# A decoder block on one core: the indexer gets two steps per z tile, and the modulation's loads move from the z tiles to the output projection

## The chip, the core and the metric

One Trainium2 chip, one core. TensorE (PE) does the matmuls, VectorE (DVE), ScalarE (ACT) and GpSimd (POOL) the rest; SyncE (SP) issues the DMAs. Each engine takes its instructions in its own order and waits where an operand isn't there. The metric is the device time of one launch in microseconds (us), the median of several runs.

## The reference, cut

256 tokens, width 2048, all in float32. Only what the change touches is shown.

```python
idx_score = einsum(w_idx, relu(einsum(q_idx, k_idx)))        # the indexer, 16 heads
_, sel = lax.top_k(where(causal, idx_score, -inf), top_k)    # top_k = 64
logits = q_lat @ kv_sel + bias                               # attention over the selected keys, 16 heads
z, xbc, dt_raw, g_a, g_b = split(h @ w_in)                   # z: 4096 columns
y = ssd(conv(xbc), dt) ; y = rms_norm(y * silu(z))
merged = sigmoid(g_a) * (y_a @ w_proj_a) + sigmoid(g_b) * (y_b @ w_proj_b)
x1 = x + gate1 * (merged @ w_out)
x2 = x1 + gate2 * swiglu(norm(x1) * (1 + scale2) + shift2)
# the six modulation vectors (gates, scales, shifts) are silu(c) @ w_ada + b_ada: 2048 x 12288
```

The selection is done here as a mask: eight rounds of "take the 8 largest of a row, strike them out" (MAX and MATCH_REPLACE), and what was struck out stays.

## The kernel before, in words

**Jobs.** The program is a list of jobs, each with one 1 MB weight tile. A tile is loaded into one of a few `raw` buffers (L144, on SP), split into a high part `wh` (ScalarE, L196) and the remainder `wl` (VectorE, L197), and multiplied on TensorE: `wh` against both parts of the activations side by side (L278, 512 columns) and `wl` against the high part (L280, 256 columns). Loads run three buffers ahead, splits two jobs ahead (`AHEAD`). Four PSUM accumulators and four side banks turn over. The scheduler of the framework sets each engine's order from the order of the code and its own estimate.

**Side work.** `gens` holds generators; a job calls `advance()` `ticks` times, spread over its matmuls (L161), and each call takes one step of each generator. The indexer, `index_gen` (L727), starts with the first z tile: eight steps of a pair of heads (`ix`, L737 and L739; relu L742; weighted sums L745 and L747), one for the causal mask on GpSimd (L752, L753), four of two top-k rounds (L758, L759), and a last one (L762, then L763 and L764 on GpSimd). The attention pairs open with a `drain` of what is left of it (`open_a2`, L595).

**Stages around the change.** Nine z tiles (`ZLEAD`, columns of z; z0 to z8) go ahead of the attention pairs. Then pair j (its q, k, v) and a z tile take turns, eight times. The two heads of a pair come one job later: logits `lg` (L873, L874), GpSimd adds mask and bias (L877, L878; the bias is loaded by L915 into `t1` from a table in DRAM), maxima L883, exponentials L886 on ScalarE, scaling L890, transposes `pT` (L894). A z tile is emptied by ScalarE (L296) and VectorE (`zs`, L297), gated with L860 and L861 (`zt`), and stored (L862, `d_z`). Later follow the projection of the attention (pa), convolution and state-space groups (cv) with the first part of their projection (pb), the rest of pb, and the output projection (out0 to out15). In the last pb jobs VectorE merges each of 16 blocks with L1180 and L1181, and with L300 and L301 (`mg`) makes the operand of the output projection; out0's matmuls take the blocks in turn, and so wait for the last `mg`.

**Granules of the modulation.** 48 of the weight tiles of `w_ada` (1 MB each, a "granule") are taken by VectorE, not TensorE: each half of a tile is scaled by a value of silu(c) and added to `acc2` (L556; the first half of a group starts it with L554). Eight granules make half a vector; after the eighth, `finish` sums over the partitions with 8 products of 128x1 on TensorE (L534; the trace has 16 records, since each is taken in two passes) and adds the bias (L537). `add_bg` puts a granule into the list of loads after a job; `Spread(jobs, n)` spreads n of them over a stage, by the table `BG`: lead, pairs, pa, convolution, pb. What is left then goes behind the out jobs, at most one each here. A granule takes a `raw` buffer as a weight tile does.

Of the kernel before, what the change touches and what calls it, by code (L numbers as in the profile page):

```python
# [22 lines left out]
NLEAD = 4  # L23
ONPE = (0, 1, 2, 3, 8, 10, 12)
AHEAD = 2
BG = (4, 8, 8, 24, 4)
SSD_LAG = 3
OUTC = ((0, 1), (1, 2), (2, 4), (12, 14), (4, 6), (6, 8), (14, 16), (8, 10), (10, 12))
OUTP = 12
# [20 lines left out]
def hybrid_block_kernel(  # L50
# [242 lines left out]
    def evac(acc, dst):  # L293

        lo = tmp.tile([P, L], F32, tag="ev", name="ev", bufs=3)
        act.activation(lo, acc[:, L:], AF.Copy)  # L296
        dve.tensor_tensor(dst, acc[:, :L], lo, op=ALU.add)  # L297
# [273 lines left out]
    def full(key, src, post, **kw):  # L571
        product_jobs(key, [src], [(0, k) for k in range(KT)], hr, lambda m, acc: post(acc), **kw)
# [282 lines left out]
    def add_z(j, ticks=1):  # L855
        def post(acc):
            v = tmp.tile([P, L], F32, tag="zv", name="zs")
            evac(acc, v)
            th = tmp.tile([P, L], F32, tag="zt", name="zt")
            act.activation(th, v, AF.Tanh, scale=0.5)  # L860
            dve.scalar_tensor_tensor(th, th, 1.0, v, op0=ALU.add, op1=ALU.mult)  # L861
            nc.sync.dma_start(d_z[j], th)  # L862

        full(f"z{j}", w_z[j], post, ticks=ticks, wide=True)
# [267 lines left out]
    def add_pb(q, mp, pre=None, ticks=1):  # L1132
        def post(m, acc):
            pb = B["pb"][:, m]
            if q == 0:
                act.activation(pb, acc, AF.Copy)
                return
            if q < 3:
                dve.tensor_tensor(pb, acc, pb, op=ALU.add)
                if q == 2:  # L1140
                    merge_most(m, pb)
            else:
                merge(m, pb, acc)

        def rhs(k):
            g = 2 * q + k // 4
            while g not in B["done"]:
                advance()
            return B["y"][g][:, k % 4]

        order = [(2 * mp + m, k) for m in range(2) for k in range(8)]
        product_jobs(f"pb{q}_{mp}", [w_pb[8 * q + mp]], order, rhs, post, pre=pre, ticks=ticks, pref=merge_load if q >= 2 else None)
# [161 lines left out]
    zs = iter(range(32))  # L1314
# [11 lines left out]

    sp = Spread(ZLEAD, BG[0])
    for i in range(ZLEAD):
        add_z(next(zs))
        sp()  # L1330
    first_pair = len(jobs)
    sp = Spread(28 - ZLEAD, BG[1])
    for j in range(8):
# [4 lines left out]
    for _ in range(12 - ZLEAD):  # L1338
        add_z(next(zs))
        sp()  # L1340
    sp = Spread(16, BG[2])
    for m in range(16):
# [3 lines left out]
    nz = 20  # L1346
    sp = Spread(48, BG[3])
    for g in range(8):
# [9 lines left out]
        if g >= 4:  # L1358
            add_pb(*next(pbs))
    sp = Spread(16, BG[4])  # L1360
    for q, mp in pbs:
# [156 lines left out]
```

## Time and profile before

| | |
|---|---|
| median of 3 runs | 1997.14 us (1996.43 to 1997.53) |
| profiled execution | 2000.2 us, span 1998.5 us |
| granted TensorE clock | 0.995 |
| TensorE busy | 98% of the span |
| VectorE, ScalarE busy | 73%, 53% |

Rows of the trace give the start of an instruction or of a run of equal ones, its duration, the engine, the line, the tiles (output<-inputs, buffer numbers left out) and in brackets the idle time ahead of it and what ended that. Instructions that follow each other overlap by some 0.08 us on VectorE, and TensorE's matmuls more, so the time from start to start is the work's pace. Sums of the forecast are made against the profiled execution's own times.

### The profile page before, as it was taken

The numbers are of one execution on the slowest core, as the hardware profiler recorded it, in microseconds if no ns is written. First come the engines' busy times: TensorE is split into PE (matmuls) and PEld (weight loads), VectorE is DVE, ScalarE is ACT, GpSimd is POOL, SyncE is SP. The second block draws the span as 40 slices with busy tenths as digits, with TensorE's granted clock in tenths as the row PEclk, the third lists the DMA queues.
The fourth block names the chain that finished last, engine by engine and source line by source line (L and its number), as shares of the span: only waits on it lengthen the run. The fifth ranks groups of instructions, "written<-read, shape, count | busy, mean of one in ns | idle before, by whom it ended". The sixth has DMA issues, their size and how long they took to land.

```text
span 1998.5 us, 31817 instructions
## 1 busy us (share of the span) xinstructions
PE 1968.4 (98%) x12990; PEld 1788.4 (89%) x12990; DVE 1455.4 (73%) x1804; ACT 1053.5 (53%) x1408; POOL 150.9 (8%) x145
## 2 busy tenths in 40 slices
PE   8999999999999999999999999999999999999997
PEld 7999998899888888999999988888888888888887
DVE  6877677977778999988889865668786555544443
ACT  3556755565345766666664344544444444443432
POOL 0000000310000111110114211000000000000000
PEclk9999999999999999999999999999999999999998
DMA  9888667666897677766767876467775555565552
GB/s 394 352 319 329 247 241 264 232 234 241 298 337 259 251 253 265 271 254 225 265 241 245 284 253 216 166 229 272 264 288 217 190 190 190 200 216 195 190 184 90
DMA packets 101650, 492.29 MB, mean 246 GB/s; under 512 B 10464, under 2 KB 45648, under 8 KB 46592
## 3 DMA queue, kind: packets, MB, share of 16 engines
q1 hardware_dynamic: 99840, 486.19, 67.2%
q0 software_dynamic: 704, 3.15, 0.4%
q8 instruction: 102, 1.67, 0.3%
q10 hardware_dynamic: 960, 0.92, 0.1%
q14 instruction: 44, 0.36, 0.0%
HBM read 475.44 MB, written 17.92 MB: 247 GB/s over the span
## 4 chain that ended last, share of the span: by engine, by line
PE 81%; issue 9%; DVE 5%; ACT 1%; DMA 1%; POOL 1%; SPq 1%; DVEq 0%; POOLq 0%; ACTq 0%
PE acc_gu L278 15%; PE acc_gu L280 8%; PE acc_dn L278 8%; PE acc_cv L278 7%; PE acc_z L278 4%; PE acc_dn L280 4%; PE acc_cv L280 4%; PE acc_pa L278 3%; PE acc_out L278 3%; PE cyc L826 2%; PE cyc L825 2%; PE cyc L824 2%; PE acc_z L280 2%; DVE wl L197 2%; PE acc_pa L280 1%
## 5 line engine op out<-in xcount | busy, mean ns | idle before, releaser
L197 DVE TENSOR_TENSOR wl<-raw,wh 128x2048 fp32r<-128x2048 f32 (+1 forms) x325 | 731.4, 2252 | 318.0 <-ACT wh L196 309.5
L196 ACT ACTIVATE wh<-raw 128x2048 fp32r<-128x2048 f32 (+1 forms) x325 | 605.3, 1865 | 307.4 <-PE acc_dn L278 94.9
L278 PE MATMUL acc_gu<-h,wh 128*128 128x512 f32 x1312 | 313.1, 391 | 0.0
L278 PEld LDWEIGHTS acc_gu<-h,wh 128*128 128x128 f32 x1312 | 241.1, 188 | 46.7
L278 PE MATMUL acc_cv<-h,wh 128*128 128x512 f32 x768 | 189.2, 396 | 0.0
L556 DVE SCALAR_TENSOR_TENSOR acc<-raw,cact,acc 128x1024 f32<-128x1024 f32 x120 | 160.1, 1334 | 20.4 <-DMA raw<-in_ada_dram 19.8
L280 PEld LDWEIGHTS acc_gu<-h,wl 128*128 128x128 f32 x1312 | 168.2, 191 | 6.4
L280 PE MATMUL acc_gu<-h,wl 128*128 128x256 f32 x1312 | 170.2, 283 | 0.0
L278 PEld LDWEIGHTS acc_cv<-h,wh 128*128 128x128 f32 x768 | 140.5, 188 | 29.1 <-issue 1.7
L278 PE MATMUL acc_dn<-ffact,wh 128*128 128x512 f32 x660 | 160.0, 392 | 0.0
L826 PE MATMUL cyc<-h,wl 128*128 128x256 f32 x512 | 144.8, 285 | 0.9 <-DVE wl L197 0.8
L824 PE MATMUL cyc<-h,wh 128*128 128x256 f32 x512 | 145.5, 285 | 0.0
L825 PE MATMUL cyc<-h,wh 128*128 128x256 f32 x512 | 145.3, 285 | 0.0
L236 PE MATMUL acc_pb<-y,wh 128*128 128x256 f32 x512 | 143.9, 281 | 1.3 <-DVE sgr L1180 1.3
L237 PE MATMUL acc_pb<-y,wh 128*128 128x256 f32 x512 | 143.0, 279 | 0.0
L238 PE MATMUL acc_pb<-y,wl 128*128 128x256 f32 x512 | 142.8, 279 | 0.0
L278 PEld LDWEIGHTS acc_dn<-ffact,wh 128*128 128x128 f32 x660 | 120.2, 188 | 23.1
L278 PE MATMUL acc_z<-h,wh 128*128 128x512 f32 x512 | 123.5, 393 | 0.0
L278 PEld LDWEIGHTS acc_z<-h,wh 128*128 128x128 f32 x512 | 93.8, 188 | 20.9 <-issue 2.7
L280 PEld LDWEIGHTS acc_cv<-h,wl 128*128 128x128 f32 x768 | 98.7, 191 | 4.4 <-issue 0.5
L280 PE MATMUL acc_cv<-h,wl 128*128 128x256 f32 x768 | 101.0, 283 | 0.0
L826 PEld LDWEIGHTS cyc<-h,wl 128*128 128x128 f32 x512 | 98.3, 193 | 1.5 <-DVE wl L197 1.5
(345 smaller groups left out, 3316.0 us busy)
## 6 DMA issues: line engine op xcount, KB each, us to landing
raw<-in_w_gu_dram SPq DMA_DIRECT2D x88, 1024.0 KB, 4.8
raw<-in_ada_dram SPq DMA_DIRECT2D x79, 1024.0 KB, 5.3
raw<-in_w_ssm_dram SPq DMA_DIRECT2D x48, 1024.0 KB, 4.8
raw<-in_w_dn_dram SPq DMA_DIRECT2D x44, 1024.0 KB, 4.7
raw<-in_w_z_dram SPq DMA_DIRECT2D x32, 1024.0 KB, 5.0
raw<-in_w_pb_dram SPq DMA_DIRECT2D x32, 1024.0 KB, 5.0
raw<-in_w_s_dram SPq DMA_DIRECT2D x30, 1024.0 KB, 5.9
raw<-in_w_pa_dram SPq DMA_DIRECT2D x16, 1024.0 KB, 6.1
```

The costliest lines, as they stand in the source:

```text
L196: act.activation(whf[:, o], raw[:, o], AF.Copy)
L197: dve.tensor_tensor(wlf[:, o], raw[:, o], whf[:, o].bitcast(F32), op=ALU.subtract)
L236: pe.matmul(acc, wh, rhs[:, :L], start=first, stop=False)
L237: pe.matmul(acc, wh, rhs[:, L:], start=False, stop=False)
L238: pe.matmul(acc, wl, rhs[:, :L], start=False, stop=last)
L278: pe.matmul(acc, wh[:, t], rhs(k), start=n == 0, stop=False, skip_group_check=True)
L280: pe.matmul(acc[:, :L], wl[:, t], rhs(k)[:, :L], start=False, stop=n == end, skip_group_check=True)
L556: dve.scalar_tensor_tensor(a, r, cact[:, k : k + 1], a, op0=ALU.mult, op1=ALU.add)
L824: pe.matmul(acc, wh[:, t], h[:, k, :L], start=first, stop=False, skip_group_check=True)
L825: pe.matmul(acc, wh[:, t], h[:, k, L:], start=False, stop=False, skip_group_check=True)
L826: pe.matmul(acc, wl[:, t], h[:, k, :L], start=False, stop=(c == n - 1), skip_group_check=True)
```

## The change

`BG[0]` goes from 4 to 0, and each of the nine z tiles of the lead takes two steps of the side work, where it took one. Since the 48 granules stay, each one moves four places later in the list, and the last four, for which BG has no room any more, are placed by the loop over the out jobs, behind out0 to out3.

```diff
-BG = (4, 8, 8, 24, 4)
+BG = (0, 8, 8, 24, 4)
...
     sp = Spread(ZLEAD, BG[0])
     for i in range(ZLEAD):
-        add_z(next(zs))
+        add_z(next(zs), ticks=2)
         sp()
```

The loop that places the last ones, unchanged:

```python
    for m in range(16):
        add_out(m)
        if m < 15:
            n = len(bg)
            add_bg(-(-n // (15 - m)))
```

In the changed kernel the indexer's 14 steps end with z7. Three places show what moves; numbers at the names are buffers, and the brackets name the engines or DMA queues that an instruction waits for.

TensorE and VectorE at the end of the lead, the changed kernel. First z9's matmuls, before and then changed; then VectorE from the last step of the indexer (L762) to the split for z10 (`wl87`); `zs_3626` empties z8.

```order
L278 MATMUL acc_z9_0_3732<-h_130,wh88_3545 128x512 [waits Activation_49]
...
L278 MATMUL acc_z9_0_3716<-h_130,wh84_3589 128x512 [waits DVE_49]
L278 MATMUL acc_z10_0_3854<-h_130,wh87_3712 128x512 [waits Activation_49]
...
L762 TENSOR_SCALAR sc_134<-sc_134 128x384 [waits DVE_49]
L197 TENSOR_TENSOR wl83_3543<-raw83_3403,wh83_3542 128x2048 [waits DMAHW4_49]
L861 SCALAR_TENSOR_TENSOR zt_3536<-zt_3536,zs_3532 128x256 [waits DMAHW7_49,Activation_49]
L197 TENSOR_TENSOR wl84_3590<-raw84_3474,wh84_3589 128x2048 [waits DMAHW6_49,PE_49,Activation_49]
L297 TENSOR_TENSOR zs_3579<-acc_z7_0_3546,ev_3580 128x256 [waits Activation_49]
L861 SCALAR_TENSOR_TENSOR zt_3583<-zt_3583,zs_3579 128x256 [waits DMAHW1_49,Activation_49]
L554 TENSOR_SCALAR acc2_0_0_3707<-raw86_3587,cact_108 128x1024 [waits DMAHW5_49]
L556 SCALAR_TENSOR_TENSOR acc2_0_0_3707<-raw86_3587,cact_108,acc2_0_0_3707 128x1024 [waits DVE_49]
L297 TENSOR_TENSOR zs_3626<-acc_z8_0_3593,ev_3627 128x256 [waits Activation_49]
```

Before, L762 stood behind `zs` of z8 and the split of z9, and no granule stood between `zs` of z7 and that of z8. z9's first matmul now waits for VectorE where it waited for ScalarE.

SP at the same place: before, from the load of pair 0's neighbour (`raw88`, z9) on, then the changed kernel from its load of pair 1 (`raw85`) on.

```order
L144 DMA raw88_3478<-in_w_z_dram 128x2048 [waits DMAHW7_49,DMAHW3_49,DVE_49]
L144 DMA raw89_3482<-in_w_att_dram 128x2048 [waits DMAHW6_49,DVE_49]
L862 DMA d_z_122<-zt_3413 128x256 [waits DMAHW5_49,DVE_49]
L144 DMA raw90_3543<-in_ada2_dram 128x2048 [waits DMAHW1_49,DVE_49]
...
L144 DMA raw85_3540<-in_w_att_dram 128x2048 [waits DMAHW2_49,DVE_49,Activation_49]
L862 DMA d_z_122<-zt_3470 128x256 [waits DMAHW1_49,DVE_49]
L915 DMA part_142<-d_tz_129 128x2x256 [waits Pool_49]
L915 DMA part_142<-d_tz_129 128x2x256 [waits DMAHW3_49,Pool_49]
L862 DMA d_z_122<-zt_3536 128x256 [waits DMAHW4_49,DVE_49]
L144 DMA raw86_3587<-in_ada2_dram 128x2048 [waits DMAHW5_49,Activation_49]
```

The two L915 (biases of pairs 2 and 3) stood behind four more loads before; now they stand ahead of the first granule's, `raw86`, and wait for GpSimd, which must have used the biases of pairs 0 and 1.

VectorE at the end of pb, the changed kernel, from the merge of blocks 10 and 11 (`sgr_11719`, `sgr_11746`) to the last `mg`; `raw255` is granule 4 of the last group, `raw257` granule 5, `wl254` the split of out0, `wl256` that of out1 (in parts).

```order
L1181 TENSOR_TENSOR pbacc_5935<-pbacc_5935,sgr_11746 128x256 [waits DVE_49,Pool_49]
L556 SCALAR_TENSOR_TENSOR acc2_1_1_10883<-raw255_11781,cact_108,acc2_1_1_10883 128x1024 [waits DMAHW6_49]
L301 TENSOR_TENSOR mg_11374<-pbacc_5935,mg_11374 128x256 [waits Activation_49] x2
L197 TENSOR_TENSOR wl254_11788<-raw254_11713,wh254_11787 128x2048 [waits DMAHW4_49]
...
L1181 TENSOR_TENSOR pbacc_5935<-pbacc_5935,sgr_11818 128x256 [waits DVE_49,Pool_49]
L556 SCALAR_TENSOR_TENSOR acc2_1_1_10883<-raw255_11781,cact_108,acc2_1_1_10883 128x1024
L301 TENSOR_TENSOR mg_11374<-pbacc_5935,mg_11374 128x256 [waits Activation_49] x2
L197 TENSOR_TENSOR wl256_11860<-raw256_11785,wh256_11859 128x512 [waits DMAHW7_49]
...
L1181 TENSOR_TENSOR pbacc_5935<-pbacc_5935,sgr_11896 128x256 [waits DVE_49,Pool_49]
L556 SCALAR_TENSOR_TENSOR acc2_1_1_10883<-raw257_11853,cact_108,acc2_1_1_10883 128x1024 [waits DMAHW6_49]
L301 TENSOR_TENSOR mg_11374<-pbacc_5935,mg_11374 128x256 [waits Activation_49] x2
```

None of the three L556 stood in this stretch before; the L534 and L537 of the group, which did, are now in out3, behind two of its matmuls.

## Rows read from the trace of the kernel before

**Rows 1.** The page: busy time, share of the span, instructions.

```profile
PE 1968.4 (98%) x12990; PEld 1788.4 (89%) x12990; DVE 1455.4 (73%) x1804; ACT 1053.5 (53%) x1408; POOL 150.9 (8%) x145
```

**Rows 2.** What TensorE waited for: us in total, times, longest.

```profile
PE acc_out L278 <- DVE mg L301: 1.5, 2, 1.3
...
PE py L1097 <- DVE ar L1060: 1.0, 1, 1.0
```

**Rows 3.** Timeline of TensorE from z7 to pair 2: start, duration; z7 (with one index step), z8 (with none), pair 0, z9, z10, the transposes, a q of pair 2.

```profile
342.23 3.94 PE L278 MATMUL acc_z<-h,wh 128*128 128x512 f32 x16
...
348.86 3.94 PE L278 MATMUL acc_z<-h,wh 128*128 128x512 f32 x16
...
354.55 0.28 PE L236 MATMUL acc_q<-cqs,wh 128*128 128x256 f32 x1
...
360.21 3.80 PE L278 MATMUL acc_z<-h,wh 128*128 128x512 f32 x16
...
372.73 3.80 PE L278 MATMUL acc_z<-h,wh 128*128 128x512 f32 x16
...
380.51 0.33 PE L894 MATMUL pT<-ident,part 128*128 128x128 f32 x1 [0.77 <-DVE part L890]
381.26 0.90 PE L894 MATMUL pT<-ident,part 128*128 128x128 f32 x5 [0.42 <-DVE part L890]
...
384.47 0.38 PE L236 MATMUL acc_q<-cqs,wh 128*128 128x256 f32 x1 [0.90 <-DVE mx L883]
```

**Rows 4.** Timeline of VectorE in the same stretch.

```profile
348.17 2.29 DVE L197 TENSOR_TENSOR wl<-raw,wh 128x2048 fp32r<-128x2048 f32 x1 [1.78 <-ACT wh L196]
350.38 1.40 DVE L747 SCALAR_TENSOR_TENSOR sc<-rl,wi,sc 128x128 f32<-128x128 f32 x4
...
352.03 0.72 DVE L758 MAX8 m<-sc 128x8 f32<-128x128 f32 x2
...
353.64 0.61 DVE L758 MAX8 m<-sc 128x8 f32<-128x128 f32 x2
...
354.81 0.61 DVE L758 MAX8 m<-sc 128x8 f32<-128x128 f32 x2
...
367.12 0.35 DVE L762 TENSOR_SCALAR sc<-sc 128x384 f32<-128x384 f32 x1
367.39 2.29 DVE L197 TENSOR_TENSOR wl<-raw,wh 128x2048 fp32r<-128x2048 f32 x1
```

**Rows 5.** Timeline of GpSimd: the causal mask, the last mask, and the bias adds of heads 0, 1 and 3.

```profile
351.46 0.47 POOL L752 TENSOR_SCALAR_AFFINE_SELECT sc<-sc 128x128 f32<-128x128 f32 x1 [116.69 <-DVE sc L747]
...
367.54 2.28 POOL L763 TENSOR_SCALAR_AFFINE_SELECT sc<-sc 128x128 f32<-128x128 f32 x1 [15.26 <-DVE sc L762]
369.78 0.39 POOL L764 TENSOR_SCALAR_AFFINE_SELECT sc<-sc 128x256 f32<-128x256 f32 x1
370.15 0.45 POOL L877 TENSOR_TENSOR part<-part,sc 128x128 f32<-128x128 f32 x1
370.57 0.74 POOL L878 TENSOR_TENSOR part<-part,sc 128x256 f32<-128x256 f32 x1
...
373.92 2.78 POOL L878 TENSOR_TENSOR part<-part,sc 128x256 f32<-128x256 f32 x1
```

**Rows 6.** Timeline of TensorE from `finish` in pb to out3.

```profile
1143.98 1.84 PE L534 MATMUL ada<-ones,acc 128*128 128x1 f32 x16
...
1156.41 0.51 PE L278 MATMUL acc_out<-mg,wh 128*128 128x512 f32 x1 [0.19 <-DVE mg L301]
1158.21 0.50 PE L278 MATMUL acc_out<-mg,wh 128*128 128x512 f32 x1 [1.29 <-DVE mg L301]
...
1170.14 3.84 PE L278 MATMUL acc_out<-mg,wh 128*128 128x512 f32 x16
```

**Rows 7.** Timeline of VectorE at the end of pb.

```profile
1143.22 0.75 DVE L1180 SCALAR_TENSOR_TENSOR sgr<-sgr,acc_pb 128x256 f32<-128x256 f32 x2
...
1146.08 2.29 DVE L197 TENSOR_TENSOR wl<-raw,wh 128x2048 fp32r<-128x2048 f32 x1 [1.43 <-ACT wh L196]
1148.29 0.75 DVE L301 TENSOR_TENSOR mg<-pbacc,mg 128x256 fp32r<-128x256 f32 x2
...
1152.63 1.89 DVE L197 TENSOR_TENSOR wl<-raw,wh 128x512 fp32r<-128x512 f32 x3
...
1157.74 0.42 DVE L301 TENSOR_TENSOR mg<-pbacc,mg 128x256 fp32r<-128x256 f32 x1
```

**Rows 8.** Timeline of SP's issues: in the pairs, and at the end of pb (the load at 1140.13 and the next are those of out1 and out2).

```profile
377.42 0.46 SPq L144 DMA_DIRECT2D raw<-in_w_att_dram  x1
...
1140.13 3.24 SPq L144 DMA_DIRECT2D raw<-in_w_out_dram  x2
```

**Rows 9.** DMA issues: count, KB each, median us from issue to landing. Each row is of a window with one granule or one weight tile: issued at 343.85 and 394.21 (behind two L915) in the lead and the pairs, and at 1140.13 (out1).

```profile
raw<-in_ada_dram SPq DMA_DIRECT2D x1, 1024.0 KB, 5.0
...
raw<-in_ada_dram SPq DMA_DIRECT2D x1, 1024.0 KB, 7.5
...
raw<-in_w_out_dram SPq DMA_DIRECT2D x1, 1024.0 KB, 7.1
```

**Rows 10.** All L554 of the program: min/median/max duration in ns.

```profile
L554 DVE TENSOR_SCALAR acc<-raw,cact x8: 743/746/753, 293.1 to 1424.1; 128x1024 f32<-128x1024 f32 x8
```

**Rows 11.** Timeline of VectorE near 1060.

```profile
1056.93 1.28 DVE L556 SCALAR_TENSOR_TENSOR acc<-raw,cact,acc 128x1024 f32<-128x1024 f32 x1
...
1061.80 2.83 DVE L197 TENSOR_TENSOR wl<-raw,wh 128x2048 fp32r<-128x2048 f32 x1
```

**Rows 12.** Timeline of ScalarE: its half of the split of out0.

```profile
1144.13 1.91 ACT L196 ACTIVATE wh<-raw 128x2048 fp32r<-128x2048 f32 x1 [2.90 <-PE acc_pb L237]
```

## The prediction

> **What bounds the kernel now.** The page's busy times come first: TensorE (PE) works 1968.4 of 1998.5 us, no other engine nearly as long [rows 1]. So a change counts only where TensorE waits or gets other work. Next the waits of TensorE: the longest outside the program's start is at the end of the mixer, where `acc_out` waits for the merged tile `mg` of L301 [rows 2], and three more stand together at the start of the attention pairs. Then the timeline at these places.
>
> In the pairs, `pT` is held twice (0.77 and 0.42 us) by L890 of VectorE (DVE) and `acc_q` once (0.90) by L883 [rows 3]. VectorE's rows say why: the top-k rounds, 1.17 us each, start only at 352.03, after the last z of the lead, and L762, which ends them, stands at 367.12 [rows 4]. The mask then goes through GpSimd (POOL): L763, L764, and two bias adds a head from 370.15 on [rows 5]. In the nine z tiles themselves TensorE shows no wait: z8 starts at 348.86, pair 0 at 354.55, z9 at 360.21 [rows 3].
>
> In the output projection TensorE reaches the last two blocks of out0 before `mg` is there (waits of 0.19 and 1.29); the last `mg` starts on VectorE at 1157.74 and TensorE's block at 1158.21 [rows 6, 7].
>
> **The change, part by part.** The instructions are the same ones (no matmul is added or dropped); they move.
>
> *Two steps per z.* The 14 steps of the indexer now end in z7. TensorE's index matmuls only change z jobs: 0. VectorE reaches L762 about 21 us earlier. Worked out back from z8's start, which doesn't move: z4 to z7 hold no index matmuls now and take 5.69 us each like z8, so z3, with the last index step, ends at 348.86 - 4 x 5.69 = 326.1 [rows 3]. With relu and the split that runs then, VectorE takes up the last scores near 327.8 and goes on without a hole: 1.40 for the scores, eight rounds of 1.17, two splits `wl` of 2.29 (2.2 to the next start) [rows 4], and seven ops on 256 columns like the 0.42 of L301 (0.34 to the next start) [rows 7]. L762 then ends at about 346.0. The mask and four heads' biases are then ready long before the logits of z9. So the waits of 0.77, 0.42 and 0.90 go: **-2.1 us**. Ends of matmuls overlap, so the start-to-start gain may reach 2.6; at least nothing is lost here.
>
> *No granule in the lead.* What is late next? z9. In the order of the changed kernel z9's first matmul waits for VectorE instead of ScalarE, and the op meant is `zs` of z8, since z9 now takes the accumulator of z8. On VectorE that `zs` stands behind L554 and L556 of the first granule (buffer 86). On SP (the DMA queue) the load of 86 stands behind two L915, which wait for GpSimd's bias adds of heads 1 and 3. Walked through:
> - L763 starts at 346.1 together with the `wl` of pair 0. In before it took 2.28 us beside a `wl`, while L752 took 0.47 [rows 4, 5]. Here it ends near 348.3, L764 (0.39) at 348.7, the first add (0.45) at 349.2.
> - The first L878 meets the `wl` of z9 (from 348.9, when z7's matmuls are done, to 351.1). A row of before has 2.78 for that instead of 0.74 [rows 5]. It ends at about 351.2; three heads of 0.45 + 0.74 follow: 354.7.
> - L915 that waits for head 3, then a `d_z`, then the load: 355.7 (about 0.4 per issue [rows 8]).
> - A granule of the lead landed 5.0 us after issue; one behind two L915 took 7.5 [rows 9]. I take 5.0, since a quarter-size load is ahead and not two full ones: 360.7.
> - L554 0.75, L556 1.28, `zs` 0.42, less their overlap of some 0.08 each [rows 7, 10, 11]: 363.0.
>
> z9 is due at 360.21, and behind it waits all of TensorE's order: **+2.8 us**. Bounds: 0 if the load is issued before 353; 5.3 with a landing of 7.5. Queued behind the waiting L554 on VectorE: `zs` of z8, the split for pair 1, and by them ScalarE's evacuations of pair 0, which the logits of z9 need; the logits come behind the first half of z9, so its own delay covers them. The second granule stands in the same way ahead of `zs` of z9; but z10 waits for ScalarE alone, as it takes the accumulator of pair 1's q, so that hold is not passed on in the sum.
>
> *The other granules* sit where the one four places earlier sat; in the convolution VectorE has the same work per job. One place differs: near 1060, a first half of a group (L554, 0.75) replaces L556 (1.28), and the second half moves ahead of L1060 [rows 10, 11]. So 0.75 + 1.28 stand ahead of it where 1.28 stood; the split between them, 2.83 there beside GpSimd's work and 2.29 elsewhere, may give 0.5 back. TensorE waits for this L1060 [rows 2]: **+0.3** (0 to 0.75).
>
> *Last four granules beside out0 to out3.* Before, VectorE was free for 1.43 ahead of the split of out0 at 1146.08 [rows 7]. Now the first half of granule 4 stands ahead of the split of out0. Its load has the place in SP's order where that of out1 stood, 1140.13, and that one landed after 7.1 us [rows 8, 9]: 1147.2. From there VectorE goes without a hole: half a granule 1.2, two `mg` 0.7, split of out0 2.2, four L1180/L1181 1.4, second half 1.2, two `mg` 0.7, four part splits 2.5, four L1180/L1181 1.4, a half of granule 5 1.2, then the last two `mg`, 0.7 [rows 7]. 1147.2 + 13.2 = 1160.4 as the end, where before it was 1158.16: **+2.3** (0.2 with a landing after 5.0 us [rows 9]; up to 3 if four ops that hang on each other leave gaps).
>
> The group's `finish` (L534, 16 matmuls, 1.84 us) leaves the place ahead of the last pb job [rows 6]. There TensorE had slack, as it waited for `mg` afterwards, so its going earns 0. It now stands inside out3, from 1170.14 before, where TensorE has no wait [rows 6]: **+1.84**. It also waits for the last half granule. On VectorE that one stands behind the split of out3, whose load SP issues when granule 5 has been used, at 1161.6: 5.0 to land [rows 9], 1.9 for ScalarE's half of the split [rows 12], 2.2, an L1214 of 0.4, and two halves of 1.2 give 1173.5. out3 is due there at 1170.14 + 2.3 + two blocks of 0.24 = 1172.9 [rows 6]: **+0.6** (0 to 3 if that load is slower).
>
> **Sum.** -2.1 + 2.8 + 0.3 + 2.3 + 1.84 + 0.6 = +5.7 us. The profiled execution took 2000.2 (span 1998.5, 1.7 around it), so that one would come to 2005.9; it was 3.06 above the median of the runs, 1997.14. Forecast for the median: **2002.8**.
>
> **A rule weighed.** What decides z9 is whether GpSimd stands still while VectorE splits. L763 took 2.28 us beside a `wl` of 2.29 and ended 0.14 after it; the same kind of op alone took 0.39 to 0.74 [rows 4, 5]. The Trainium skill ("SBUF — State Buffer", section "SBUF: two separate sides") says that VectorE, for an op with two SBUF inputs, and GpSimd take one shared port pair as an exclusive lock, for the whole instruction, so that the other blocks fully. By that rule the trace agrees, and the sum is the one above. Without it the ten ops would take 0.47 + 0.39 + 4 x 1.19 = 5.6 us, 86 would be issued near 352.7 and z9 would not wait: the sum would be +2.9.
>
> **The rivals.**
> - *z9 doesn't wait* (GpSimd less held, or 86 issued before 353): 1997.14 - 2.1 + 0.3 + 4.7 = **2000.0**. For it: the z lead has slack everywhere else. Against: the rows of 2.28 and 2.78.
> - *The loads land late*, each after the slowest row, 7.5 us [rows 9]. z9 then waits 5.3. The second granule's load waits on SP for `zt` of z8 (365.6 + 2.5 late = 368.1), lands at 375.6, and its first half (1.2) stands ahead of the op that ScalarE needs before it can empty pair 1's q (1.5), whose accumulator z10 takes: 378.3, where z10 is due at 365.5 + 12.5 = 378.0 by the spacing of z9 and z10 [rows 3]: 0.3. Granule 4 is 0.4 later and out3's load 2.5. Sum 5.7 + 2.5 + 0.3 + 0.4 + 2.5 = 11.4, **2008.5**. For it: SP has two L915 shortly before. Against: those are a quarter of the size each.
> - *No granule is waited for* (the other side). If 86 lands by 357.9 and granule 4 by 1144.65 (4.5 after issue; 5.0 is a row [rows 9]), the halves fall into VectorE's holes, z9 and the last `mg` keep their times, and `finish` alone costs: -2.6 + 1.84 = -0.8, **1996.4**.
> - *The change doesn't do what it says*: the indexer's two steps don't bring the top-k ahead, as VectorE is full in the lead. It idles 1.78 ahead of a split there [rows 4], and loses four granules' eight halves; hardly.
>
> **How the numbers follow.** Forecast 0.55, z9 not waiting 0.2, late loads 0.15, no granule waited for 0.1. 0.2% is 4 us here, about what a measurement of this kernel can tell from no change. The range takes in the first two, with z9's wait anywhere from 0 to 5.3, and reaches towards the third and fourth: 1998.0 to 2007.0. Slower by over 0.2% (past 2001.1): most of the forecast and the third, 0.63; within: 0.32; faster 0.05, since no case gives 4 us.
>
> **What would show it.** Right: no wait of `pT` or `acc_q` near 380; a wait of `acc_z` for `zs` of 2 to 4 us just after pair 0; L763 near 346; a load of the first granule issued near 356; the last `mg` about 2 us after its place relative to out0's load; L534 inside out3 with a wait of 0.5 to 1. Wrong: z9 starting right after pair 0, L534 without a wait, or a new wait in the index steps of z1 to z3, where ScalarE's L742 and the four side banks now turn over twice as fast. What would make it wrong above all is a landing time: both big terms hang on when one 1 MB load lands.

## The result, and the profile after

| | before | changed |
|---|---|---|
| median of the runs | 1997.34 us (1996.43 to 2000.84, 4 runs) | 2012.31 us (2009.5 to 2013.89, 4 runs) |
| profiled execution, span | 2000.2 us, 1998.5 us | 2011.46 us, 2009.8 us |
| granted TensorE clock in it | 0.995 | 0.994 |

The ratio is 1.0073, with an interval of 1.0061 to 1.0085: **slower by about 14.6 us**, where 5.7 were forecast and the range ended at 2007.0. The sign was right, the size was not.

The busy times of the page hardly differ from [rows 1]:

```profile
PE 1969.9 (98%) x12990; PEld 1787.3 (89%) x12990; DVE 1456.0 (72%) x1804; ACT 1051.3 (52%) x1408; POOL 154.2 (8%) x145
```

The same instructions are there, and TensorE is busy 1.5 us longer. The rest is waiting. The waits of TensorE in the changed kernel (us in total, times, longest), to be read against [rows 2]:

```profile
PE acc_z L278 <- DVE zs L297: 7.5, 1, 7.5
...
PE acc_out L278 <- DVE mg L301: 3.2, 1, 3.2
PE acc_pb L236 <- DVE sgr L1180: 2.5, 3, 1.4
...
PE pT L894 <- DVE o L301: 1.1, 1, 1.1
PE py L1099 <- DVE cd L1061: 1.1, 2, 0.8
```

Where the time came in is seen from the start of the same matmuls in the two timelines:

| first matmul of | before | changed | shift | gained or lost in between |
|---|---|---|---|---|
| z0 | 294.52 | 293.06 | -1.45 | -1.45, ahead of anything that moved |
| pair 0 | 354.55 | 352.47 | -2.08 | -0.63 |
| z9 | 360.21 | 365.75 | +5.54 | **+7.62** |
| the z tile at 388.83 | 388.83 | 392.94 | +4.11 | -1.43 |
| pa, first | 492.15 | 497.51 | +5.36 | +1.25 |
| mid-convolution (its 1047th matmul) | 889.70 | 895.42 | +5.72 | +0.36 |
| out0 | 1151.42 | 1157.89 | +6.47 | +0.75 |
| the gate-up stage | 1248.07 | 1259.84 | +11.77 | **+5.30** |
| end | 1998.50 | 2009.76 | +11.25 | -0.52 |

Two places carry it: z9, and the output projection. By z0 the profiled execution of before was already 1.45 us later than that of the changed kernel, ahead of anything that the change touches; without it the difference of the two spans is 12.7.

**z9.** Timeline of TensorE from pair 0 to z9, where [rows 3] has 354.55 and 360.21 and a duration of 3.80:

```profile
352.47 0.28 PE L236 MATMUL acc_q<-cqs,wh 128*128 128x256 f32 x1
...
358.02 0.27 PE L944 MATMUL acc_v<-wh,kvs 128*128 128x256 f32 x1
365.75 5.27 PE L278 MATMUL acc_z<-h,wh 128*128 128x512 f32 x16 [7.46 <-DVE zs L297]
```

TensorE stands still for 7.46 us, and then the 16 matmuls, which took 3.80 before, take 5.27. The table of short stretches gives the reason (stretch and its length; busy time and count of PE, PEld, DVE, ACT and POOL; then the granted clock, the DMA engines' share and GB/s):

```profile
361.00:362.00 1.00, 0.00 (x0) 0.00 (x0) 0.00 (x0) 0.00 (x0) 0.00 (x0) 0.92 0.74 254
362.00:363.00 1.00, 0.00 (x0) 0.00 (x0) 0.00 (x0) 0.00 (x0) 0.00 (x0) 0.50 0.98 377
...
367.00:368.00 1.00, 1.00 (x3) 0.77 (x3) 1.00 (x2) 1.00 (x3) 0.00 (x0) 0.50 0.78 311
368.00:369.00 1.00, 1.00 (x4) 0.80 (x3) 0.23 (x1) 1.00 (x1) 0.00 (x0) 0.66 1.01 426
369.00:370.00 1.00, 1.00 (x6) 0.79 (x5) 0.44 (x1) 0.53 (x1) 0.00 (x0) 1.00 0.91 318
```

The granted clock falls to 0.50 (1.2 GHz of 2.4) during the wait and stays there for the first 2.9 us of work after it: 3 matmuls a microsecond instead of 6. That is the 1.5 us.

What z9 waited for, link by link. GpSimd, to be read against [rows 5]:

```profile
345.31 4.82 POOL L763 TENSOR_SCALAR_AFFINE_SELECT sc<-sc 128x128 f32<-128x128 f32 x1 [16.07 <-DVE sc L762]
...
354.44 0.73 POOL L878 TENSOR_TENSOR part<-part,sc 128x256 f32<-128x256 f32 x1
```

VectorE in the same stretch, against [rows 4]:

```profile
344.89 0.35 DVE L762 TENSOR_SCALAR sc<-sc 128x384 f32<-128x384 f32 x1
345.16 2.29 DVE L197 TENSOR_TENSOR wl<-raw,wh 128x2048 fp32r<-128x2048 f32 x1
347.36 0.42 DVE L861 SCALAR_TENSOR_TENSOR zt<-zt,zs 128x256 f32<-128x256 f32 x1
347.69 2.29 DVE L197 TENSOR_TENSOR wl<-raw,wh 128x2048 fp32r<-128x2048 f32 x1
349.90 0.42 DVE L297 TENSOR_TENSOR zs<-acc_z,ev 128x256 f32<-128x256 f32 x1
...
363.29 0.75 DVE L554 TENSOR_SCALAR acc<-raw,cact 128x1024 f32<-128x1024 f32 x1 [12.06 <-DMA raw<-in_ada_dram]
364.08 1.28 DVE L556 SCALAR_TENSOR_TENSOR acc<-raw,cact,acc 128x1024 f32<-128x1024 f32 x1
365.28 0.42 DVE L297 TENSOR_TENSOR zs<-acc_z,ev 128x256 f32<-128x256 f32 x1
```

SP, where the two L915 wait for GpSimd and the granule's load stands behind them:

```profile
352.97 2.59 SPq L915 DMA_DIRECT2D part<-d_tz  x2
355.66 0.42 SPq L862 DMA_DIRECT2D d_z<-zt  x1
356.19 0.36 SPq L144 DMA_DIRECT2D raw<-in_ada_dram  x1
```

And that load, issue to landing, beside [rows 9]:

```profile
raw<-in_ada_dram SPq DMA_DIRECT2D x1, 1024.0 KB, 7.1
```

The chain is the one that the forecast walked through; two links are longer. L763 is held not over one `wl` but over the `wl`, the `zt` and the next `wl`, which follow each other without a hole, and ends 0.15 after the second (350.13 and 349.98). The bias adds then run to 355.17. The load takes 7.1 us, not 5.0, and VectorE, which has nothing else that it may do, idles 12.06.

**The output projection.** VectorE at the last `mg`, to be read against [rows 7]:

```profile
1153.25 1.28 DVE L556 SCALAR_TENSOR_TENSOR acc<-raw,cact,acc 128x1024 f32<-128x1024 f32 x1 [0.94 <-DMA raw<-in_ada_dram]
...
1164.27 1.28 DVE L556 SCALAR_TENSOR_TENSOR acc<-raw,cact,acc 128x1024 f32<-128x1024 f32 x1
1165.46 0.75 DVE L301 TENSOR_TENSOR mg<-pbacc,mg 128x256 fp32r<-128x256 f32 x2
```

TensorE there, against [rows 6]:

```profile
1165.94 0.83 PE L278 MATMUL acc_out<-mg,wh 128*128 128x512 f32 x2 [3.17 <-DVE mg L301]
...
1167.07 5.41 PE L278 MATMUL acc_out<-mg,wh 128*128 128x512 f32 x16
...
1180.51 1.92 PE L534 MATMUL ada<-ones,acc 128*128 128x1 f32 x16 [0.19 <-DVE acc L556]
```

From 1153.25 to the last `mg` VectorE has no hole: the half granules and the splits between them push `mg` back, as forecast, and TensorE waits 3.17 in one piece where it waited 0.19 and 1.29. Behind this wait, too, 16 matmuls take 5.41 instead of 3.84, at half clock:

```profile
1167.00:1168.00 1.00, 1.00 (x5) 0.85 (x5) 1.00 (x3) 0.22 (x1) 0.00 (x0) 0.70 0.44 155
1168.00:1169.00 1.00, 1.00 (x4) 0.73 (x3) 1.00 (x3) 0.00 (x0) 0.00 (x0) 0.50 0.69 131
```

### The profile page after: what moved, and what is told of

Read it like the earlier page. It is cut to its first block, busy times and chain, and to the rows that moved or that the text cites. A ratio compares the mean times of both kernels' runs of the same rounds, so it can differ in the third digit from the quotient of the medians.

```text
span 2009.8 us, 31828 instructions
## 1 busy us (share of the span) xinstructions
PE 1969.9 (98%) x12990; PEld 1787.3 (89%) x12990; DVE 1456.0 (72%) x1804; ACT 1051.3 (52%) x1408; POOL 154.2 (8%) x145
## 4 chain that ended last, share of the span: by engine, by line
PE 78%; issue 9%; DVE 7%; DMA 3%; ACT 3%; POOL 1%; SPq 1%; DVEq 0%; POOLq 0%; ACTq 0%
PE acc_gu L278 15%; PE acc_gu L280 8%; PE acc_dn L278 8%; PE acc_cv L278 7%; PE acc_z L278 4%; PE acc_dn L280 4%; PE acc_cv L280 3%; PE acc_pa L278 3%; DVE wl L197 3%; PE acc_out L278 2%; PE acc_z L280 2%; PE cyc L826 2%; PE cyc L825 2%; PE cyc L824 2%; PE acc_pa L280 1%
## 5 line engine op out<-in xcount | busy, mean ns | idle before, releaser
L556 DVE SCALAR_TENSOR_TENSOR acc<-raw,cact,acc 128x1024 f32<-128x1024 f32 x120 | 162.0, 1350 | 29.6 <-DMA raw<-in_ada_dram 29.2
L236 PEld LDWEIGHTS acc_pb<-y,wh 128*128 128x128 f32 x512 | 96.1, 188 | 3.5 <-issue 1.9
```

Source lines behind the costliest of these rows:

```text
L236: pe.matmul(acc, wh, rhs[:, :L], start=first, stop=False)
L556: dve.scalar_tensor_tensor(a, r, cact[:, k : k + 1], a, op0=ALU.mult, op1=ALU.add)
```

## The experiments

The theory after the result: z9's wait comes from the order on SP. The earlier top-k brings the two L915 up ahead of the next loads, and they hold SP until GpSimd, itself held by VectorE's splits, has used the biases. Rivals: it is the granule ahead of `zs` (so that moving granules is needed for it); VectorE is full in the lead; or the output projection is where most of the time goes. All ratios below are to the kernel before, measured on the same chip.

### One part alone: two steps per z, the granules as before

```diff
-BG = (0, 8, 8, 24, 4)
+BG = (4, 8, 8, 24, 4)
```

> One half of the change alone: two steps per z tile, BG left at (4, 8, 8, 24, 4). Theory (z9 waits because the first granule's load stands on SP behind two L915 that wait for GpSimd): the granules of the lead are loaded long before, so z9 has no wait of zs; the waits of pT and acc_q near 380 go (-2.1); the L915 now stand ahead of the load of pair 1's weights, which may make pair 1 wait up to 2. The output projection is as before. 1995 to 1998, out stage within 0.5 of before. Rival (the two steps themselves fill VectorE so that zs of z8 is late): acc_z waits for zs by 5 or more, 2003 or above.

Measured: 2004.15 us, ratio 1.0027 (1.0017 to 1.0038). Missed: 1995 to 1998 was expected, with no wait of z9. The waits near 380 are gone, but z9 waits just as long, with no granule between the `zs` of z7 and that of z8. TensorE, then ScalarE and VectorE, then SP:

```profile
367.42 6.63 PE L278 MATMUL acc_z<-h,wh 128*128 128x512 f32 x16 [7.53 <-ACT part L923]
```

```profile
364.91 1.91 ACT L196 ACTIVATE wh<-raw 128x2048 fp32r<-128x2048 f32 x1 [11.34 <-DMA raw<-in_w_att_dram]
```

```profile
366.86 2.29 DVE L197 TENSOR_TENSOR wl<-raw,wh 128x2048 fp32r<-128x2048 f32 x1 [10.66 <-ACT wh L196]
```

```profile
357.24 0.38 SPq L915 DMA_DIRECT2D part<-d_tz  x1
...
359.46 0.37 SPq L915 DMA_DIRECT2D part<-d_tz  x1
359.93 0.41 SPq L144 DMA_DIRECT2D raw<-in_w_att_dram  x1
```

Here the load behind the two L915 is pair 1's weights, and the op that z9 waits for is L923, which stands behind the split of those weights on ScalarE. VectorE idles 10.66, so it isn't full. The granule isn't needed for the wait: whatever load comes behind the two L915 is late. z9's matmuls take 6.63, again at half clock.

### The other part alone: one step per z, the granules as changed

```diff
-        add_z(next(zs), ticks=2)
+        add_z(next(zs))
```

> The other half alone: BG (0, 8, 8, 24, 4), one step per z. Theory: the indexer ends late as before, so GpSimd's mask and the L915 come after the first granule's load on SP; no wait of z9; the waits of pT and acc_q near 380 stay; the output projection costs about 5 as in the changed kernel. 2001 to 2004. Rival (moving the granules is enough to make z9 wait): acc_z waits 5 or more there, 2009 or above.

Measured: 2004.41 us, ratio 1.0033 (1.0020 to 1.0045). z9 doesn't wait (359.00, right behind pair 0), the waits of `pT` and `acc_q` near 380 stay, and the loss is in the output projection:

```profile
1155.42 1.17 PE L278 MATMUL acc_out<-mg,wh 128*128 128x512 f32 x2 [3.17 <-DVE mg L301]
```

The clock behind it is 0.50 from 1156 to 1158 and 0.54 in the next microsecond. A second stretch of 0.50, from about 1172.6 to 1176, follows L534, which hardly waited (0.11), and the 14 matmuls of out3 behind it take 5.06, where the changed kernel took 3.47:

```profile
1169.89 1.92 PE L534 MATMUL ada<-ones,acc 128*128 128x1 f32 x16
1171.67 5.06 PE L278 MATMUL acc_out<-mg,wh 128*128 128x512 f32 x14
```

So the four granules in the output projection are a loss by themselves, of 6.6 us by the ratio, where the forecast had 4.7 for this stage. The two parts together, 0.27% and 0.33%, are 0.60% of the 0.73%.

### The changed kernel with L915 issued from GpSimd's own queue

```diff
-            nc.sync.dma_start(t1, bass.AP(s.tensor, s.offset + 127, [[383, P], [P * 384, 2], [1, L]]))
+            nc.gpsimd.dma_start(t1, bass.AP(s.tensor, s.offset + 127, [[383, P], [P * 384, 2], [1, L]]))
```

> The changed kernel, with the eight loads of the bias (L915) issued by GpSimd instead of SP, so that nothing on SP waits for GpSimd. Theory: the first granule is loaded some 10 us earlier, lands before VectorE asks for it, z9 starts right after pair 0, and the slower clock behind that wait is gone too: 8 to 9.5 less than the changed kernel, 2002 to 2005. Rival (the granule's place on VectorE or its slow landing is the cause, not SP's order): z9 still waits 3 or more, 2007 or above.

Measured: 2001.33 us, ratio 1.0015 (1.0006 to 1.0024), 11.0 below the changed kernel's median (11.6 by the two ratios). GpSimd is held exactly as long as in the changed kernel:

```profile
345.16 4.82 POOL L763 TENSOR_SCALAR_AFFINE_SELECT sc<-sc 128x128 f32<-128x128 f32 x1 [16.07 <-DVE sc L762]
```

but SP issues the granule's load 8.8 us earlier, it lands after 5.0, and z9 comes right behind pair 0 at full clock:

```profile
347.35 0.33 SPq L144 DMA_DIRECT2D raw<-in_ada_dram  x1
```

```profile
raw<-in_ada_dram SPq DMA_DIRECT2D x1, 1024.0 KB, 5.0
```

```profile
357.96 3.80 PE L278 MATMUL acc_z<-h,wh 128*128 128x512 f32 x16
```

So the hold on GpSimd costs nothing by itself; it costs by what waits behind it on SP. The `acc_out` wait stays, at 3.4, and L534 has a stretch of 0.50 behind it here too (14 matmuls in 5.04).

### The same edit in the kernel before, a control

The kernel before, with that line alone changed.

> The kernel before with L915 issued by GpSimd, a control. Theory: SP was not held by L915 there, since the indexer ended late and four loads were ahead; the waits of pT and acc_q near 380 stay: same as before within 1.5. Rival (GpSimd's queue is worth something by itself, so that e3 and e5 prove nothing of the change): 3 or more under before.

Measured: 1996.96 us, ratio 0.9999 (0.9990 to 1.0008). The queue of L915 is worth nothing where the top-k comes late. So the 11.0 of the third experiment belong to the changed order.

Its trace shows something else. VectorE's order at the end of pb is that of before, yet the waits of TensorE on `acc_out`, 1.5 in [rows 2], aren't there: the list of waits from pb's end to the gate-up stage holds only

```profile
PE n2b L364 <- DVE rcol L345: 0.8, 1, 0.8
```

and its execution takes 2.9 us less than that of before from mid-convolution to the gate-up stage. In the two other versions that keep the granules' old places `acc_out` waits 0.7 in all, and this stretch takes 2.8 (two steps per z) and 2.2 less (that with L915 on the other queue, below). So the profiled execution of before was a long one just there. Near 380 the control also differs: `acc_q` waits its 0.90 but `pT` doesn't wait, and from z9's start to the z tile at 388.83 it takes 1.26 less than before, though its top-k comes as late. VectorE's order is not quite the same there (a `zs` stands ahead of an L890), so this may be the order or the execution.

### The changed kernel with its last four granules behind out3 to out6

```diff
-        if m < 15:
+        if 3 <= m < 15:
```

> The changed kernel, with the last four granules behind out3 to out6 instead of out0 to out3, so that none of their halves stands ahead of the last mg on VectorE. Theory: acc_out waits for mg 1.0 to 1.8 as before instead of 3.2, and the slower clock behind it (about 1.2) goes; finish (1.84) stays: 2.5 to 3.5 less than the changed kernel, 2008 to 2010; z9 waits as in the changed kernel. Rival (the output projection's loss is finish and load traffic, not VectorE's order): less than 1 gained.

Measured: 2010.29 us, ratio 1.0061 (1.0049 to 1.0074). `acc_out` still waits 2.3 in all (0.86 and 1.44), with no granule ahead of the last `mg` on VectorE, which had waited 1.12 for the load of a `sgr`. No half clock follows these waits. But L534, further down, waits longer, and there the half clock follows (0.50 from 1196 to 1199): 16 matmuls take 5.52:

```profile
1163.70 0.50 PE L278 MATMUL acc_out<-mg,wh 128*128 128x512 f32 x1 [1.44 <-DVE mg L301]
...
1193.42 1.95 PE L534 MATMUL ada<-ones,acc 128*128 128x1 f32 x16 [1.19 <-DVE acc L556]
1195.23 5.52 PE L278 MATMUL acc_out<-mg,wh 128*128 128x512 f32 x16
```

The gain over the changed kernel is about 2 us by the medians, and the two intervals overlap. In the traces the stretch from mid-convolution to the gate-up stage is 3.1 shorter than in the changed kernel (2.96 longer than before's, where the changed kernel has 6.05), and all of that is won ahead of out0: from out0 on it loses 5.55, the changed kernel 5.30. z9's wait is there as it was, but its 16 matmuls take 6.65, not 5.27: the half clock behind the same wait lasted longer in this execution.

### Both edits: L915 from GpSimd's queue, and the granules later

> The changed kernel with L915 issued by GpSimd and the last four granules behind out3 to out6 (e3 and e4 together). Theory (VectorE's three halves ahead of the last mg cost 2 to 2.5, and the clock that falls behind that wait 1.2 to 1.9 more; finish and its own wait remain): acc_out waits under 2, granted clock 1.00 through out0 and out1, 2.5 to 4 less than e3, 1997.5 to 1999. Rival (the out jobs lose by finish and loads alone): within 1 of e3.

Measured: 2000.68 us, ratio 1.0011 (1.0002 to 1.0019). Missed: it is the same as without the second edit, as the rival said. `acc_out` waits 0.2 and 1.3 as before, and the wait has moved on:

```profile
1182.13 3.58 PE L534 MATMUL ada<-ones,acc 128*128 128x1 f32 x16 [3.33 <-DVE acc L556]
```

```profile
1188.00:1189.00 1.00, 1.00 (x4) 0.81 (x3) 1.00 (x1) 0.57 (x2) 0.49 (x1) 0.50 0.66 115
```

L534 waits 3.33 for the last half granule. The clock falls to 0.50 during this wait, at 1181, and stays there to 1191: L534 takes 3.58, not 1.92, and the 16 matmuls behind it 6.55. From mid-convolution to the gate-up stage it takes 6.67 longer than before, and the third experiment 6.32. In both places that were tried a granule in the output projection costs: it delays `mg`, or it holds L534.

### Two steps per z, the granules as before, L915 from GpSimd's queue

```diff
-BG = (0, 8, 8, 24, 4)
+BG = (4, 8, 8, 24, 4)
```

and the edit of L915.

> Two steps per z, BG left at (4, 8, 8, 24, 4), and L915 issued by GpSimd. Theory (the wait of z9 in e1 too comes from L915 on SP): no wait of acc_z for L923, no slow clock there, no waits of pT and acc_q near 380, the output projection as in e1: 7 to 9 less than e1, 1994 to 1997, at or under before. Rival (e1's wait comes from somewhere else, as no granule stood in the way there): acc_z waits 5 or more, 2002 or above.

Measured: **1994.98 us, ratio 0.9985 (0.9973 to 0.9996)**, the one version that is below both kernels. z9 starts at 359.12 right behind pair 0, the waits near 380 are gone, and `acc_out` waits 0.7. The span of the profiled execution is 1991.1, its clock 0.996. What is left in the stages that the forecast spoke of:

```profile
PE acc_pb L236 <- DVE sgr L1180: 2.7, 2, 1.6
...
PE acc_out L278 <- DVE mg L301: 0.7, 1, 0.7
```

The gain of 1.8 by the medians (0.8 to 5.4 by the interval) is what the forecast gave to the top-k's waits, 2.1; in the trace it is 2.9 between z9's start and the z tile at 388.83 (a shift of -1.09 turns into -3.99) against the profiled execution of before, and 1.6 against the control's.

### The last four granules in the projection of the attention

The version above with `BG = (4, 8, 12, 24, 0)`.

> As e5, with the four granules of the pb jobs moved to the pa jobs: BG (4, 8, 12, 24, 0). VectorE is busy 73% in pa and 88% from pb's end on, and TensorE waits only in the latter. Theory (granules cost nothing where VectorE has slack and the load has time): the last mg comes earlier, acc_out waits under 1, and pb's wait of sgr is smaller: 1 to 3 less than e5, 1992 to 1996. Rival (pa's loads, which run at 0.86 of the DMA engines, get late): waits of L278 in pa for ScalarE's split, 2 or more above e5.

Measured: 1999.21 us, ratio 1.0013 (1.0004 to 1.0022). Missed: new waits stand elsewhere. The first is in the lead, where the granules stand as in the version above:

```profile
305.38 0.49 PE L737 MATMUL ix<-kT,part 64*128 64x128 f32 x4 [2.04 <-ACT kT L726]
```

A load makes it: the tile of z issued at 292.58 landed after 7.3, where the version above has it issued at 292.62 and landing after 5.1. Its split on ScalarE starts at 300.03, not 297.87, and L860 and `kT` follow that much later. The clock falls to 0.50 behind this wait. The order up to there is the same in both versions, so this part of the loss may be one execution's, and it says nothing of the granules. The second is at the start of the convolution, where the first split waits with four more granules ahead, and a wait of 0.88 has the half clock behind it (5.50 for 16 matmuls):

```profile
585.42 5.50 PE L278 MATMUL acc_cv<-h,wh 128*128 128x512 f32 x16 [0.88 <-ACT wh L196]
```

`acc_out` still waits 2.7 in all.

## Why the prediction was wrong, step by step

- **Two steps per z, -2.1: the mechanism was right.** `pT` and `acc_q` don't wait near 380; L762 stands at 344.89, forecast near 346. From z9's start to the z tile at 388.83 the shift falls by 1.43 although 1.47 of slow matmuls lie in between, so the gain is 2.9, as in the fastest version. Set against the control, which has the late top-k too, the gain is 1.6, near the 1.8 that the fastest version gained by its medians. So how much of the 2.9 is the top-k's stays open. The lead itself, from z0 to pair 0, took 0.63 less, where the forecast had 0; in the other versions with two steps it took 0.5 to 0.6 less.
- **z9's wait, +2.8: this step failed.** It measured 7.46. Put on one clock (the changed execution ran 1.45 early, so add 1.45 to its times), L763 starts at 346.8 (forecast 346.1) and ends at 351.6 (348.3): it was held over two splits and not over one, +2.5. The adds behind it met little of a split, which gave 1.3 back: the load was issued at 357.6 (355.7). It landed after 7.1, not 5.0: +2.1. VectorE's three ops took 0.15 more, and z9 was due 0.5 earlier than assumed. In sum 0.7 + 2.5 - 1.3 + 2.1 + 0.15 + 0.5 = 4.65, which with the 2.8 makes the 7.46. The upper bound that was kept for this wait, 5.3, was too low, since it varied the landing alone.
- **The clock was in no term.** Each microsecond of a long wait was priced at a microsecond. By the duration of the 16 matmuls behind the two long waits, 5.27 - 3.80 and 5.41 - 3.84, the half clock cost 1.5 and 1.6 more.
- **Last mg +2.3, finish +1.84, its wait +0.6.** The mechanism was right: the half granules alone reproduce it in the second experiment. The wait in [rows 2], 1.5, grew to 3.17; L534 took 1.92 and waited 0.19; with the slow clock that is 1.7 + 2.1 + 1.6 = 5.4, and the stage measured 5.30, where 4.74 were forecast. That L534 and its wait cost about what was forecast (2.2 from start to start, 2.44 forecast) is luck of this execution: in the second, third, fifth and sixth experiments they cost 3.8, 3.8, 4.9 and 9.7, by the half clock and the waits.
- **The base was wrong too.** The 3.06 by which the profiled execution of before stood above its median were taken off at the end, as if they lay away from the terms. 1.45 of them is the stretch ahead of z0 (0.8 against the control), but 1.9, from start to start against the control, was at the wait of `acc_out`, which the control and two other versions with the same order have at 0 and 0.7. A typical execution loses more by the granules than this trace shows: set against the control, the stretch from mid-convolution to the gate-up stage is 6.05 + 2.89 = 8.9 longer in the changed kernel, and 4.24 + 2.89 = 7.1 in the second experiment, whose ratio says 6.6.
- **Smaller ones.** `py` waits 2.2 in all, where it waited 1.8, near the +0.3 that was forecast. `acc_pb` waits 2.5 in all (1.3 before), and a `pT` wait of 1.1 appears at 460.51: neither was in the sum. Ahead of that `pT` VectorE waited 4.18 for a granule (both its halves, 2.60, then a split, then the L301 it hangs on). With the granules later in the output projection, and the same order in this place, VectorE waited 3.50 for that granule and `pT` not at all, so it hangs on when one load lands.
- **The rivals.** "Loads land late" (2008.5) came nearest, with a granule at 7.1, but for z9 only: granule 4 landed after 5.4. "No granule waited for" and "z9 doesn't wait" fell; the second is what the third experiment makes by hand, and its 2001.33 stands beside the 2000.0 that was worked out for it, though its output projection lost 6.3 (from mid-convolution on) and not 4.7.

**The rule weighed** held in its direction. The Trainium skill ("SBUF — State Buffer", section "SBUF: two separate sides") has the port pair locked for a whole instruction. The trace agrees, as GpSimd's L763 was held over the whole of a `wl`, and shows more: L763 did not get through at two turns, between `wl` and `zt` and between `zt` and the next `wl`, and ended only when VectorE took up `zs`, which has one operand in PSUM. It is not always so: in the first experiment and in the fastest version L763 lasted 1.61, over a half granule and a `zt`, and ended 0.15 after the `zt`, though another half granule followed at once. The forecast counted one instruction where a row of three followed each other.

## What to carry to other kernels

When work that frees a buffer is moved earlier, look on the DMA queue for the transfer that refills this buffer: it moves up too, and if it waits for its releaser, every load behind it waits with it; a queue of its own took away 11.0 us here and cost nothing in the control. A wait on TensorE should be priced with the half-clock stretch that may follow, another 1.5 us or more here, and it followed a wait of 0.88 and L534 without a wait to speak of; and a wait that the profile shows once is not yet the typical one: a second execution shows which it is. And work that is put into a stage without holes has a price wherever in the stage it goes: four granules lost about 6.6 us there when they alone were moved, and moving them three jobs further moved the wait without a gain (with L915 on its own queue).

## What the hardware showed that wasn't expected

- **The clock behind a wait.** From z0 on, TensorE's waits of 2.04, 3.17 (twice), 3.33, 3.38, 7.46, 7.48 and 7.53 us all had a granted clock of 0.50 in the matmuls behind them. The length of the wait alone doesn't tell: a wait of 2.85 at the program's start (changed kernel, 18.55) was followed by a clock of 1.00; a wait of 0.88 (last experiment) had the 0.50 behind it, the 1.44 of the fifth and the 1.61 of the first (`acc_pb`, 1127.09) did not, and behind L534 it came after waits of 0.11, 0.13 and 1.19 but not after the 0.19 of the changed kernel. In the changed kernel at z9 the clock had fallen before work resumed; at `acc_out` it was still 1.00 when the matmuls began and fell 1.4 us later. The same wait of 7.5 cost 1.5 in one execution and 2.8 in two others (16 matmuls in 5.27, 6.63 and 6.65). The Trainium skill ("TensorE: Matmul & The Clock Gate", Part 1) says that the throttled 1.2 GHz is the default state and that activity releases it. The 0.50 behind the long waits agrees, while ahead of the 0.50 behind L534 in the second and third experiments TensorE had waited only 0.11 and 0.13.
- **A GpSimd instruction of 0.4 us lasted 4.82** while three VectorE instructions with both operands in SBUF followed each other: in the changed kernel and in the third, fifth and sixth experiments, which have the same order there.
- **A 1 MB load took 5.0 or 7.1 us** at nearly the same place. The 5.0 had no bias transfer ahead of it in SP's queue, the 7.1 had two of 256 KB within 3.2 us, and came again in the fifth experiment with the same order (7.08); but in the first experiment a load right behind one took about 5.0 too (359.93 to the split's start at 364.91), and the load of the lead in the last experiment took 7.3, where the same one took 5.1 in another version, with no bias transfer near. So what makes the difference stays open.
- **The same order of instructions, another wait.** The waits of `acc_out` were 1.5, 0.7, 0.7 and 0 in four profiled executions with the same order at that place.
